# A first feed-forward pass shared by three token tiles instead of two, on eight cores

## The chip, the cores and the metric

The kernel runs on all eight cores of one Trainium2 chip. Each core works on its own two sequences with the same program and nothing is exchanged. The metric is the device time of the slowest core, in microseconds (us).

The runs of these kernels show a second, slower state: in some executions the cores of one die, or of both, show a lower granted TensorE clock and the run is longer (the milder ones 0.92 to 0.94 on one die and about 2990 us, the worst ones 0.81 to 0.82 and about 3300 us, against 2855 us for before in the fast state).

## The reference, cut to what matters

One decoder layer over x of shape (16, 2048, 1024): a half-step SwiGLU feed-forward network (FFN 1), a token mixer (differential attention beside latent attention, one output projection), a second half-step FFN (FFN 2), a final norm. Every part is normed and modulated by shift, scale and gate, which are products of c and `w_ada`.

```python
u = modulate(rmsnorm(h, ffn1_norm[l]), sh1, sc1)
h = h + 0.5 * g1 * swiglu(u, ffn1_w_gate[l], ffn1_w_up[l], ffn1_w_down[l])   # FFN 1
u = modulate(rmsnorm(h, mix_norm[l]), sh2, sc2)
h = h + g2 * hybrid_mixer(u, cos_d, sin_d, cos_r, sin_r, l, ...)              # mixer
u = modulate(rmsnorm(h, ffn2_norm[l]), sh3, sc3)
h = h + 0.5 * g3 * swiglu(u, ffn2_w_gate[l], ffn2_w_up[l], ffn2_w_down[l])   # FFN 2
```

## The kernel before: the parts that the change touches

A core has eight tiles of 512 tokens, numbered 0 to 7. The FFN weights (about 17 MB in bf16 for one FFN) do not stay on chip. They stream through a ring of six buffers `wf`. The first use of a block reads 1 MB of f32 through the POOL queue, converts it on the way and stores a bf16 copy in DRAM; each later use reloads 512 KB.

```python
def load(self, src, scr, key, cols=2048, reuse=True, after=None):
    i = self.i % len(self.bufs); self.i += 1
    buf, res = self.bufs[i], self.res[i]
    if key not in self.seen:                       # first use: f32, POOL queue
        self.seen[key] = Res(f"scr{key}")
        G.dma("pool", f"{self.name}c{i}", 128 * cols * 4, w=[res], after=after, out=buf[:, 0:cols], in_=src[:, 0:cols])
        if reuse:
            G.dma("sp", f"{self.name}s{i}", ..., r=[res], w=[self.seen[key]], out=scr[:, 0:cols], in_=buf[:, 0:cols])
    else:                                          # later: bf16, SP queue
        G.dma("sp", f"{self.name}{i}", 128 * cols * 2, r=[self.seen[key]], w=[res], out=buf[:, 0:cols], in_=scr[:, 0:cols])
    return buf, res
```

Because first loads are slow (8.0 us from issue to landing for a first `w_gu` block on the page of before, 4.9 us for a reload), tiles 0 and 1 go through FFN 1 together (the joint pass): every pair of weight blocks is used for both tiles. Tile 1 borrows memory of the mixer, which is idle then.

```python
def gate_up(fi, hook=None, joint=False):
    sets = [(uF, uFR, ACTV, actR)] + ([(uF1, uF1R, ACT1, act1R)] if joint else [])
    for fp in range(11):                           # 11 feature pairs
        tg, tgR = wf.load(w_gu[fi, fp, 0], ...)
        tu, tuR = wf.load(w_gu[fi, fp, 1], ...)
        for c in range(2):
            for u, uR, av, aR in sets:
                ...                                # 16 matmuls 128x512, then ACT, DVE, DVE
        if hook: hook(fp)                          # modulation blocks, conversions

def down_first(b):
    held = []
    for mp in range(4):
        held.append(down_load(0, mp))              # three w_dn blocks
        down_use(0, mp, held[mp], 0, b, bank=jb)
        if mp < 2: down_use(0, mp, held[mp], 1, b, ACT1, act1R, jb)
    gate.append(G.ops[-1])                         # the mixer's w_in may be loaded
    for mp in (2, 3): down_use(0, mp, held[mp], 1, b, ACT1, act1R, jb)
```

After the joint pass, tile 0 leaves: its mixer input is normed, its state is spilled, tile 2's x is loaded into its place and normed. Then tile 2's FFN 1 and tile 0's mixer run side by side, and so on. Three kinds of side work fill the passes: modulation blocks (`ada`, 1 MB of f32 each, blocks 20 to 23 being the gate of the mixer), conversions of FFN 2's weights ahead of use (`convert`, 1 MB read and 512 KB written each), and the mixer's own first-time weights (`w_in`, `w_uq`, `w_out`).

```python
early = [8, 9, 10, 11, 16, 17, 18, 19, 12, 13, 14, 15]     # modulation blocks in the joint pass
late = list(range(20, 36))
ahead = {3: 5, 4: 5, 5: 5, 6: 5, 7: 5}                      # conversions by tile
def hook_f(x):
    def hook(fp):
        if x == 2 and fp % 2 == 0 and fp < 8 or x > 2 and fp in (1, 5, 8):
            if late: ada(late.pop(0), fb)
        if fp % 2 == 0 and fp // 2 < ahead.get(x, 0): convert([rest.pop(0)])
    return hook
n2(0, A, 1.84, True); n2(1, B, 2.0, True)                   # tiles 0 and 1 leave
load_x(2, A); norm(1, 2, A, 1.95); load_x(3, B)             # (within segments)
```

The numbers 1.84, 2.0 and so on are priorities: a list scheduler in the program fixes each engine's order of instructions at build time, with its own model of durations and transfers.

The softmax here doesn't subtract the row's maximum and nothing guards it: scores larger than these inputs give would overflow.

## Time and profile before

| | before |
|---|---|
| time, median of 4 runs | 2854.95 us (2853.25 to 3221.71; the last one is slow) |
| span of the profiled run, slowest core (7) | 2875.9 us; median of the first die's cores 2845.7 us |
| TensorE busy (core 7) | 2728.7 us, 95% |
| HBM read | 498.70 MB |

These lines are from the page of the profiled run of before: busy time and share of an engine, the span in 40 slices (tenths busy, tenths of full clock, DMA share), the HBM total and the issues of reloads (count, KB of each, us to landing).

```profile
PE 2728.7 (95%) x15753; PEld 1356.6 (47%) x15753; DVE 1492.9 (52%) x2829; ACT 1225.7 (43%) x2034; POOL 599.5 (21%) x565
...
PE   3999789999999999999999999999999999999998
...
PEclk8889999999999999999999999999999999999999
DMA  9678889886885967857547695566564655434553
...
HBM read 498.70 MB, written 112.51 MB: 213 GB/s over the span
...
wf<-s_gu SPq DMA_DIRECT2D x308, 512.0 KB, 4.9
wf<-s_dn SPq DMA_DIRECT2D x106, 512.0 KB, 3.8
...
wf<-s_dn SPq DMA_DIRECT2D x53, 384.0 KB, 3.8
```

TensorE is full nearly everywhere. There are two dents: the first slice (PE is busy for 23.7 of the first 72 us of core 1, while the first weights and x arrive) and slices 5 and 6, where the joint pass hands over to the tile-by-tile part. Core 7 is not the best core to study: cores 6 and 7 had a granted clock of 0.81 from about 76 to 237 us in this run. Core 1 did not. The next lines are the windows view of core 1: from:to, length, busy us of PE, PEld, DVE, ACT and POOL with instruction counts, then the granted clock, the DMA share and GB/s.

```profile
0.00:72.00 72.00, 23.71 (x199) 10.48 (x200) 23.15 (x57) 21.53 (x30) 8.31 (x19) 0.82 0.97 196
72.00:310.00 238.00, 235.40 (x1235) 108.05 (x1234) 94.35 (x147) 50.38 (x78) 26.98 (x46) 0.99 0.88 183
310.00:400.00 90.00, 66.31 (x328) 29.27 (x327) 54.48 (x64) 29.63 (x48) 35.52 (x32) 0.83 0.82 217
400.00:1500.00 1100.00, 1059.28 (x6438) 540.71 (x6436) 598.22 (x1192) 541.52 (x911) 257.62 (x238) 0.99 0.75 211
1500.00:2780.00 1280.00, 1260.61 (x7276) 636.10 (x7275) 699.92 (x1337) 574.22 (x957) 270.43 (x232) 1.00 0.57 183
```

The third line is the handoff: PE is idle for 90.00 − 66.31 = 23.7 us of it. The timeline of PE on core 1 shows why (start, length, instruction, count, and in brackets the idle time before and what ended it):

```profile
318.62 0.79 PE L317 MATMUL psall<-ar,onesf 128*128 128x512 f32 x1 [4.70 <-POOL ar L317]
...
329.74 0.61 PE L317 MATMUL psall<-ft,onesb 128*128 128x512 bf16 x1 [1.96 <-ACT ft L317]
336.99 1.46 PE L317 MATMUL psall<-ft,onesb 128*128 128x512 bf16 x3 [6.64 <-DVE ft L317]
344.55 1.44 PE L317 MATMUL psall<-uF,wf 128*128 128x512 bf16 x3 [6.10 <-ACT uF L317]
```

PE waits for sums of squares in the mixer (`ar`), for the squares of tile 2's x (`ft`), which is still arriving, and then for the normed tile 2 (`uF`).

### The profile page before, as it was taken

Reading aid. Unit: us, or ns where it says so; the run is one execution under the profiler, and the core shown is the slowest. Engines: PE = TensorE matmul, PEld = TensorE weight load, DVE = VectorE, ACT = ScalarE, POOL = GpSimd, SP = SyncE. Lnnn points to the kernel's source line nnn. Section 1 sums busy time; section 2 is a strip of 40 time slices with the busy share of each in tenths; the row PEclk is TensorE's granted clock in tenths of the full one; section 3 lists DMA queues with packets and bytes.
Section 4 is the critical chain, followed back from the end, with each engine's and each line's share of the span. In section 5 each row is a group of like instructions: output and inputs, shape, how many; then the busy total and the mean of one; then the engine's idle time right before and its main releaser. Section 6 shows DMA issues by size and latency. Waiting matters only on the chain.

```text
span 2875.9 us, 40104 instructions; the slowest of 8 cores (2837.4 to 2875.9 us)
## 1 busy us (share of the span) xinstructions
PE 2728.7 (95%) x15753; PEld 1356.6 (47%) x15753; DVE 1492.9 (52%) x2829; ACT 1225.7 (43%) x2034; POOL 599.5 (21%) x565
## 2 busy tenths in 40 slices
PE   3999789999999999999999999999999999999998
PEld 1444344445544454455554444554455545555443
DVE  3333467565546544554336685565654565434443
ACT  3210325335623665246663353464255533566211
POOL 1011220241312203313023123220222212210110
PEclk8889999999999999999999999999999999999999
DMA  9678889886885967857547695566564655434553
GB/s 199 144 153 176 243 187 219 217 242 198 247 240 158 256 184 223 243 177 228 171 145 234 166 268 196 166 207 195 184 187 133 225 173 179 157 125 162 180 184 116
DMA packets 169773, 552.67 MB, mean 192 GB/s; under 512 B 17648, under 2 KB 34416, under 8 KB 160112
## 3 DMA queue, kind: packets, MB, share of 16 engines
q1 hardware_dynamic: 152304, 488.91, 52.8%
q0 software_dynamic: 17280, 61.19, 13.8%
q8 instruction: 125, 2.05, 0.3%
q14 instruction: 64, 0.52, 0.1%
HBM read 498.70 MB, written 112.51 MB: 213 GB/s over the span
## 4 chain that ended last, share of the span: by engine, by line
PE 80%; DVE 10%; DMA 7%; ACT 2%; issue 1%; POOL 1%; SPq 0%; DVEq 0%; POOLq 0%; ACTq 0%
PE psall L317 80%; DMA wf<-s_gu 2%; DMA mix<-w_ada 1%; DVE mt L317 1%; DVE junk L317 1%; DVE pt L317 1%; DVE h L317 1%; DVE bt L317 1%; DVE mix L317 1%; DMA h<-xT 1%; DVE nt L317 1%; DMA s_h<-mt 1%; DVE ft L317 1%; DMA wm<-w_out 1%; DMA wf<-s_dn 1%; DVE rec L317 1%
## 5 line engine op out<-in xcount | busy, mean ns | idle before, releaser
L317 PE MATMUL psall<-uF,wf 128*128 128x512 bf16 x5280 | 1436.9, 384 | 30.1 <-DVE ft L317 9.9
L317 PEld LDWEIGHTS psall<-uF,wf 128*128 128x128 bf16 x5280 | 502.3, 99 | 554.1 <-issue 71.6
L317 PE MATMUL psall<-actv,wf 128*128 128x512 bf16 x2640 | 730.7, 379 | 2.7 <-DMA wf<-s_dn 2.7
L317 ACT ACTIVATE pt<-psall 128x512 bf16<-128x512 f32 (+3 forms) x896 | 488.2, 560 | 366.1 <-PE psall L317 363.2
L317 ACT ACTIVATE ft<-psall 128x512 f32<-128x512 f32 x352 | 209.7, 597 | 635.3 <-PE psall L317 628.5
L317 DVE SCALAR_TENSOR_TENSOR ft<-ft,psall 128x512 f32<-128x512 f32 x352 | 240.2, 684 | 394.4 <-ACT ft L317 393.6
L317 PEld LDWEIGHTS psall<-actv,wf 128*128 128x128 bf16 x2640 | 248.9, 98 | 246.9 <-DMA wf<-s_dn 3.2
L317 PE MATMUL psall<-mix,pt 128*128 128x129 bf16 x3264 | 329.8, 221 | 21.6 <-DVE pt L317 15.8
L317 PEld LDWEIGHTS psall<-mix,pt 128*128 128x128 bf16 x3264 | 248.7, 98 | 215.2 <-DVE pt L317 34.1
L317 DVE TENSOR_TENSOR actv<-ft,psall 128x512 bf16<-128x512 f32 x330 | 226.0, 685 | 230.7 <-PE psall L317 227.9
L317 PE MATMUL psall<-uM,wm 128*128 128x512 bf16 x896 | 302.6, 384 | 6.2 <-ACT mt L317 4.0
L317 POOL TENSOR_TENSOR sq<-h 128x512 f32<-128x512 f32 x175 | 189.9, 1093 | 388.8 <-DVE h L317 375.7
L317 DVE SCALAR_TENSOR_TENSOR h<-psall,SC,h 128x512 f32<-128x512 f32 x128 | 95.9, 749 | 317.4 <-PE psall L317 317.2
L317 POOL TENSOR_TENSOR ac<-h 128x512 f32<-128x512 f32 x25 | 30.1, 1205 | 903.3 <-DVE h L317 596.2
L317 PE MATMUL psall<-mix 128*128 128x512 bf16 x576 | 209.5, 367 | 0.2 <-ACT pt L317 0.2
L317 POOL TENSOR_TENSOR ac<-ac,sq 128x512 f32<-128x512 f32 x150 | 199.0, 1327 | 8.5
L317 DVE TENSOR_TENSOR mt<-tab,psall 128x512 f32<-128x512 bf16 (+1 forms) x208 | 139.6, 683 | 74.2 <-ACT bt L317 55.5
L317 DVE TENSOR_TENSOR nt<-h,rs 128x512 f32<-128x512 f32 x192 | 139.7, 746 | 35.4 <-ACT rs L317 22.8
L317 PE MATMUL psall<-oT,wm 128*128 128x512 bf16 x512 | 150.8, 379 | 0.0
L317 ACT ACTIVATE bt<-psall 128x512 bf16<-128x512 f32 x104 | 61.9, 596 | 201.2 <-PE psall L317 201.0
L317 PEld LDWEIGHTS psall<-uM,wm 128*128 128x128 bf16 x896 | 87.2, 99 | 112.9 <-issue 8.6
L317 PE MATMUL psall<-mix,wf 128*128 128x512 bf16 x528 | 134.6, 413 | 0.0
(98 smaller groups left out, 2180.6 us busy)
## 6 DMA issues: line engine op xcount, KB each, us to landing
wf<-s_gu SPq DMA_DIRECT2D x308, 512.0 KB, 4.9
wf<-s_dn SPq DMA_DIRECT2D x106, 512.0 KB, 3.8
wm<-s_in SPq DMA_DIRECT2D x63, 512.0 KB, 5.0
wf<-w_gu POOLq DMA_DIRECT2D x44, 512.0 KB, 8.0
s_gu<-wf SPq DMA_DIRECT2D x44, 512.0 KB, 7.8
wf<-s_dn SPq DMA_DIRECT2D x53, 384.0 KB, 3.8
s_h<-h SPq DMA_DIRECT2D x16, 1024.0 KB, 6.7
mt<-s_h SPq DMA_DIRECT2D x64, 256.0 KB, 5.2
```

What stands on the lines that cost most here:

```text
L317: ins = getattr(eng, o.fn)(**o.kw)
```

## The change

The intent: let tile 2 join the first pass. Its state and its FFN memory lie in memory that belongs to the mixer's scratch (`mix2`: attention outputs, latents, probabilities, temporaries, rope table), all idle until the pass is over. The weights are then reloaded one pass fewer. In the down pass the tiles leave one by one, so that the first tile's mixer can start while the others still give TensorE work. Four modulation blocks (20 to 23) and four conversions move into the longer joint pass. The core of the diff (memory plan and renames cut):

```diff
         def gate_up(fi, hook=None, joint=False):
-            sets = [(uF, uFR, ACTV, actR)] + ([(uF1, uF1R, ACT1, act1R)] if joint else [])
-            for fp in range(11):
+            sets = [(uF2, uF2R, ACT2, act2R), (uF, uFR, ACTV, actR), (uF1, uF1R, ACT1, act1R)] if joint else [...]
+            steps = [(0, 1)] + [(fp,) for fp in range(2, 11)] if joint else [(fp,) for fp in range(11)]
...
-        def down_first(b):
+        def down_first():
+            sets = [(2, ACT2, act2R), (1, ACTV, actR), (0, ACT1, act1R)]
+            two = Rot([0, 1])
             held = []
             for mp in range(4):
                 held.append(down_load(0, mp))
-                down_use(0, mp, held[mp], 0, b, bank=jb)
-                if mp < 2:
-                    down_use(0, mp, held[mp], 1, b, ACT1, act1R, jb)
-            gate.append(G.ops[-1])
-            for mp in (2, 3):
-                down_use(0, mp, held[mp], 1, b, ACT1, act1R, jb)
+                for slot, av, aR in sets[:3 if mp < 2 else 1]:
+                    down_use(0, mp, held[mp], slot, 0, av, aR, two)
+                if mp == 1:
+                    gate.append(G.ops[-1])
+            for slot, av, aR in sets[1:]:
+                for mp in (2, 3):
+                    down_use(0, mp, held[mp], slot, 0, av, aR, two)
...
-        early = [8, 9, 10, 11, 16, 17, 18, 19, 12, 13, 14, 15]
+        early = [8, 9, 10, 11, 16, 17, 18, 19, 12, 13, 14, 15, 20, 21, 22, 23]
         def hook_j(fp):
-            for i in range(2 if fp == 9 else 1):
-                ada(early.pop(0), jb)
+            for i in range(2 if fp in (2, 4, 5, 7, 8, 10) else 1):
+                if early:
+                    ada(early.pop(0), jb)
+            if fp in (1, 3, 6, 9):
+                convert([rest.pop(0)])
...
-        late = list(range(20, 36))
-        ahead = {3: 5, 4: 5, 5: 5, 6: 5, 7: 5}
+        late = list(range(24, 36))
+        ahead = {4: 5, 5: 6, 6: 6, 7: 5}
...
-                if x == 2 and fp % 2 == 0 and fp < 8 or x > 2 and fp in (1, 5, 8):
+                if x > 3 and fp in (1, 5, 8):
```

More of the change, by code (lines that the diff above doesn't have):

```diff
@@ L413, in build, with part2 @@
         uFR = [Res(f"uF{k}") for k in range(NK)]
-        uM = sb("uM", [128, NK, 512], BF16)
+        mix2 = sb("mix2", [128, 47 * 512], BF16)
+        cut2 = [0]
+        def part2(n, dt=BF16):
+            ap = mix2[:, cut2[0]:cut2[0] + n * 512]
+            cut2[0] += n * 512
+            return ap if dt == BF16 else ap.bitcast(dt)
+        oT = part2(8).rearrange("p (h n) -> p h n", h=8)
+        uM = part2(8).rearrange("p (k n) -> p k n", k=NK)
+        qm = part2(4).rearrange("p (h n) -> p h n", h=4)
+        lat = part2(5).rearrange("p (j n) -> p j n", j=5)
+        ptiles = Rot([(part2(1), Res(f"pt{i}")) for i in range(6)])
+        mtmp = Rot([(part2(2, F32), Res(f"mt{i}")) for i in range(7)])
+        tab, tabR = part2(2).rearrange("p (i n) -> p i n", i=2), Res("tab")
+        ACT2 = mix2[:, 0:22 * 512].rearrange("p (f n) -> p f n", f=22)
+        act2R = [Res(f"act2_{f}") for f in range(22)]
+        uF2 = mix2[:, 38 * 512:46 * 512].rearrange("p (k n) -> p k n", k=NK)
+        uF2R = [Res(f"uF2_{k}") for k in range(NK)]
+        H.append(mix2[:, 22 * 512:38 * 512].bitcast(F32).rearrange("p (k n) -> p k n", k=NK))
+        HR.append([Res(f"h2_{k}") for k in range(NK)])
         uMR = [Res(f"uM{k}") for k in range(NK)]
-        onat = uM[:].rearrange("p k n -> p (k n)").bitcast(F32).rearrange("p (h q d) -> p h q d", h=4, q=4)
+        onat = uM.rearrange("p k n -> p (k n)").bitcast(F32).rearrange("p (h q d) -> p h q d", h=4, q=4)
         ACTV = sb("actv", [128, 22, 512], BF16)
@@ L438, in build @@
         uF1R = [Res(f"uF1_{k}") for k in range(NK)]
-        oT = sb("oT", [128, 8, 512], BF16)
         oTR = [Res(f"oT{h}") for h in range(8)]
-        qm = sb("qm", [128, 4, 512], BF16)
         qmR = [Res(f"qm{h}") for h in range(4)]
-        ptiles = Rot([tile(f"pt{i}", [128, 512], BF16) for i in range(6)])
-        lat = sb("lat", [128, 5, 512], BF16)
         latR = [Res(f"lat{j}") for j in range(5)]
         onatm = lat[:, 0:4, :].rearrange("p j n -> p (j n)").rearrange("p (q h d) -> p q h d", q=4, h=4)
-        tab, tabR = tile("tab", [128, 2, 512], BF16)
         WF = [sb(f"wf{i}", [128, 2048], BF16) for i in range(6)]
@@ L453, in build @@
         ntmp = Rot([tile(f"nt{i}", [128, 512], F32) for i in range(2)])
-        mtmp = Rot([tile(f"mt{i}", [128, 512], F32) for i in range(7)])
         rstmp = Rot([tile(f"rs{i}", [128, 512], F32) for i in range(2)])
@@ L478, in build @@
         colc_sb = con[:, 130:131]
-        lam_t, lamR = mtmp.items[0]
-        lam_sb = lam_t[:, 0:256].rearrange("p (i n) -> p i n", i=4)
         cTR, badaR, gainsR, gsmR, colcR = [Res(n) for n in ("cT", "bada", "gains", "gsm", "colc")]
@@ L494, in build @@
         junk, junkR = tile("junk", [128, 512], BF16)
+        lam_t, lamR = junk[:].bitcast(F32), junkR
+        lam_sb = lam_t.rearrange("p (i n) -> p i n", i=4)
         ident = cm[:, 0, :]
@@ L568, in prologue @@
         def prologue():
-            load_x(0, A, 4)
+            load_x(0, 2, 4)
             G.dma("sp", "c1", 67072, w=[cTR, badaR, gainsR, gsmR, colcR], out=con[:], in_=consts)
@@ L578, in lambdas @@
         def lambdas():
-            G.dma("sp", "c6", 131072, w=[lamR], out=lam_t[:, 0:256], in_=lamv)
+            G.dma("sp", "c6", 131072, w=[lamR], out=lam_t, in_=lamv)
             TT(lam_sb[:, 0, :], lam_sb[:, 0, :], lam_sb[:, 1, :], ALU.mult, [lamR], [lamR])
@@ L598, in mixer_init @@
             transfer(uF1R, qzR)
+            transfer(act2R, oTR + uMR + qmR)
             G.dma("pool", "c0", 3 * 65536, w=[cmR], after=after, out=cm[:].rearrange("p c n -> p (c n)"), in_=cmats)
@@ L723, in gate_up @@
             bank = jb if joint else fb
-            sets = [(uF, uFR, ACTV, actR)] + ([(uF1, uF1R, ACT1, act1R)] if joint else [])
-            for fp in range(11):
-                tg, tgR = wf.load(w_gu[fi, fp, 0], s_gu[fi, fp, 0], ("gu", fi, fp, 0))
-                tu, tuR = wf.load(w_gu[fi, fp, 1], s_gu[fi, fp, 1], ("gu", fi, fp, 1))
-                for c in range(2):
-                    f = 2 * fp + c
-                    for u, uR, av, aR in sets:
+            sets = [(uF2, uF2R, ACT2, act2R), (uF, uFR, ACTV, actR), (uF1, uF1R, ACT1, act1R)] if joint else [(uF, uFR, ACTV, actR)]
+            steps = [(0, 1)] + [(fp,) for fp in range(2, 11)] if joint else [(fp,) for fp in range(11)]
+            for step in steps:
+                tiles = {}
+                for fp in step:
+                    for i in range(2):
+                        tiles[fp, i] = wf.load(w_gu[fi, fp, i], s_gu[fi, fp, i], ("gu", fi, fp, i))
+                for u, uR, av, aR in sets:
+                    for f in range(2 * step[0], 2 * step[-1] + 2):
+                        (tg, tgR), (tu, tuR), c = tiles[f // 2, 0], tiles[f // 2, 1], f % 2
                         bg, bu = bank.next(), bank.next()
@@ L739, in gate_up @@
                 if hook:
-                    hook(fp)
+                    for fp in step:
+                        hook(fp)
         def down_load(fi, mp):
@@ L805, in load_u @@
         def load_u(t):
-            G.dma("sp", "lu", 1048576, r=[s_uR[t]], w=uMR, slack=1500.0, out=uM[:].rearrange("p k n -> p (k n)"), in_=s_u[t])
+            G.dma("sp", "lu", 1048576, r=[s_uR[t]], w=uMR, slack=1500.0, out=uM.rearrange("p k n -> p (k n)"), in_=s_u[t])
         def unspill(t, s):
@@ L1034, in build @@
         begun = [o for o in G.ops if o.dma][-1]
+        with G.seg(-0.95, -0.9, "lam", eng="dve"):
+            lambdas()
         with G.seg(-0.95, -0.9, "st1.0"):
-            st = hstats(A, jb.next())
+            st = hstats(2, jb.next())
         with G.seg(-0.8, -0.8, "N1.0"):
-            apply_norm(A, 0, 0, st, uF, uFR, ntmp)
-        with G.seg(-0.7, -0.7, "x.1", eng="sp"):
-            load_x(1, B, 4, after=begun)
-        with G.seg(-0.2, 0.0, "N1.1"):
-            st = hstats(B, jb.next())
-            apply_norm(B, 0, 0, st, uF1, uF1R, ntmp)
-        with G.seg(0.2, 0.4, "lam", eng="dve"):
-            lambdas()
-            table(0)
-        early = [8, 9, 10, 11, 16, 17, 18, 19, 12, 13, 14, 15]
-        def hook_j(fp):
-            for i in range(2 if fp == 9 else 1):
-                ada(early.pop(0), jb)
-        with G.seg(0.0, 1.333, "F1.0+1g"):
+            apply_norm(2, 0, 0, st, uF2, uF2R, ntmp)
+        for t, s, dst, dstR in ((1, 1, uF, uFR), (2, 0, uF1, uF1R)):
+            with G.seg(-0.7, -0.7, f"x.{t}", eng="sp"):
+                load_x(t, s, 4, after=begun)
+            with G.seg(-0.2, 0.0, f"N1.{t}"):
+                st = hstats(s, jb.next())
+                apply_norm(s, 0, 0, st, dst, dstR, ntmp)
+        early = [8, 9, 10, 11, 16, 17, 18, 19, 12, 13, 14, 15, 20, 21, 22, 23]
+        rest = [("gu", a, b) for a in range(11) for b in range(2)] + [("dn", a, 0) for a in range(12)]
+        def hook_j(fp):
+            for i in range(2 if fp in (2, 4, 5, 7, 8, 10) else 1):
[3 more added lines that the diff above has]
+                convert([rest.pop(0)])
+        with G.seg(0.0, 2.0, "F1.012g"):
             gate_up(0, hook_j, joint=True)
-        with G.seg(1.333, 2.0, "F1.0+1d"):
-            down_first(0)
+        with G.seg(2.0, 3.0, "F1.012d"):
+            down_first()
         gate = gate[0]
-        with G.seg(1.6, 1.9, "mixinit", eng="pool"):
+        with G.seg(2.8, 2.9, "mixinit", eng="pool"):
             mixer_init(gate)
@@ L1061, in n2 @@
             with G.seg(x, x + 0.05, f"N2.{t}"):
-                st = hstats(s, fb.next()) if fast else spread(squares(hsrcs(s), acct, sqt, accr), fb.next(), D, rstmp)
+                st = hstats(s, 2) if fast else spread(squares(hsrcs(s), acct, sqt, accr), fb.next(), D, rstmp)
                 dst, dstR = (ACTV[:, 14:22, :], actR[14:22]) if t else (uM, uMR)
@@ L1081, in norm @@
             with G.seg(lo, lo + 0.05, f"N{2 * i - 1}.{t}"):
-                st = spread(sums, fb.next(), D, rstmp) if sums else hstats(s, fb.next())
+                st = spread(sums, fb.next(), D, rstmp) if sums else hstats(s, 2)
                 apply_norm(s, 2 * i - 2, t // 4, st, uF, uFR, ntmp)
-        order = [(1, t, t % 2) for t in range(2, 8)] + [(2, t, t % 2) for t in range(8)]
-        mixers = [(0, 2.0, 3.0), (1, 3.0, 4.4), (2, 4.4, 6.2), (3, 6.2, 8.3), (4, 8.3, 9.3), (5, 9.3, 10.7), (6, 10.7, 12.5), (7, 12.5, 14.5)]
-        rest = [("gu", a, b) for a in range(11) for b in range(2)] + [("dn", a, 0) for a in range(12)]
-        late = list(range(20, 36))
-        ahead = {3: 5, 4: 5, 5: 5, 6: 5, 7: 5}
+        order = [(1, t, t % 2) for t in range(3, 8)] + [(2, t, t % 2) for t in range(8)]
+        mixers = [(0, 2.75, 3.85), (1, 3.85, 5.1), (2, 5.1, 6.7), (3, 6.7, 8.6), (4, 8.6, 9.6), (5, 9.6, 10.9), (6, 10.9, 12.5), (7, 12.5, 14.4)]
+        late = list(range(24, 36))
+        ahead = {4: 5, 5: 6, 6: 6, 7: 5}
         def hook_f(x):
             def hook(fp):
-                if x == 2 and fp % 2 == 0 and fp < 8 or x > 2 and fp in (1, 5, 8):
+                if x > 3 and fp in (1, 5, 8):
                     if late:
@@ L1099, in hook_f @@
             return hook
-        n2(0, A, 1.84, True)
-        n2(1, B, 2.0, True)
-        with G.seg(1.8, 1.85, "x.2"):
-            load_x(2, A)
-        norm(1, 2, A, 1.95)
-        with G.seg(2.0, 2.05, "x.3"):
-            load_x(3, B)
+        n2(0, 2, 2.68, True)
+        transfer(act2R + HR[2] + uF2R, latR + [tabR] + [res for _, res in ptiles.items + mtmp.items])
+        with G.seg(2.9, 3.0, "tab.0", eng="dve"):
+            table(0)
+        n2(1, 1, 2.84, True)
+        with G.seg(2.85, 2.86, "x.3"):
+            load_x(3, 1)
+        norm(1, 3, 1, 2.95)
+        n2(2, 0, 3.0, True)
+        with G.seg(3.0, 3.05, "x.4"):
+            load_x(4, 0)
+        ra(*mixers[0])
+        ra(*mixers[1])
         for n, (f, t, s) in enumerate(order):
-            x = float(n + 2)
+            x = float(n + 3)
             nxt = order[n + 1] if n + 1 < len(order) else None
@@ L1115, in build @@
                         unspill(nxt[1], nxt[2])
-                    elif nxt[1] > 3:
+                    elif nxt[1] > 4:
                         load_x(nxt[1], nxt[2])
@@ L1119, in build @@
             with G.seg(x, x + 0.667, f"F{f}.{t}g", lead=0.05):
-                gate_up(f - 1, hook_f(n + 2))
-            if n == 0:
-                ra(*mixers[0])
+                gate_up(f - 1, hook_f(n + 3))
             if t == 6 and f == 2:
```

## The prediction

> **What bounds it now.** TensorE. The page's first part gives PE 2728.7 us busy of 2875.9 (95%); the chain of waits puts 80% of the span on PE. A 128x512 matmul takes 0.216 us in the stream (44 in 9.50 us, timeline of the first down pass), 0.262 us where the granted clock is 0.81. So only PE's idle 147 us, and clock, can be won. By the windows view: 48 us idle before 72 us (weights and x arriving), about 27 us at 320 to 380 us (handoff from the joint pass to mixer 0 and tile 2), 13 us at the end, some 59 us over the middle, mostly at tile boundaries with DMA share 0.95 or more.
>
> In the handoff slot 0 is done at 314 us, leaving 19 us of down pass for slot 1. Then PE waits on stats of tile 2's x (last landed near 354 us, held further by slow DVE copies), on w_in (gated until 314 us) and on latent sums. Tile 2's gate starts at 367 us.
>
> **What the change does.**
> 1. A third tile runs in the joint pass. PE's matmuls stay the same; 33 weight reloads go (about 16.5 MB of 553); four conversions and four modulation blocks move into this pass. It gets 114 us longer (528 x 0.216), the rest 114 us shorter. Per feature pair DMA falls from 2.5 MB in 13.8 us to 3.1 MB in 20.7 us; full-clock cores already keep PE full here, so that wins nothing directly.
> 2. Tiles leave the down pass one by one: after the first, 38 us of matmuls remain instead of 19, and w_in is released 19 us before the first exit. Mixer 0's projections mix with the down passes (the program order shows it). But tile 3's x still needs slot 1's spill and norm; that step took about 40 us before. The hole shrinks from 27 to about 10 us: -17 us.
> 3. Startup: in PE's order all eight stat matmuls of the third x stand before the second tile's gate. Before, x parts landed 4.6 us apart, the last at 65.8 us; four more put the start near 78 us, against 24 extra gate matmuls (5 us) done earlier: +6 us.
> 4. The first step covers two feature pairs with four of six buffers; the next pair's second buffer frees only eight matmuls before the step ends, and a w_gu load takes 8.0 us: +4 us. Late weights of the fourth down block: +2 us.
> 5. One tile boundary fewer in the busy middle: -5 us.
>
> Aliasing adds waits (mixer scratch behind the third tile's spill, the rope table later), mostly under PE work.
>
> **Prediction.** 2854.7 - 17 + 12 - 5, about 2845 us; 8 in 10: 2822 to 2872. Faster over 2%: 0.06; within: 0.90; slower: 0.04.
>
> **What would show each step.** PE idle at the start 54 us instead of 48, waiting on ft from late x; one gap of about 4 us on wf<-w_gu some 100 matmuls later; handoff idle about 10 us instead of 27, projections among down matmuls; DMA share in the joint pass about 0.75; 33 weight reloads fewer; PE busy equal at equal clock.
>
> **What would make it wrong.** [...] cores 6 and 7 alone show 0.81, from about 72 to 236 us. If a longer joint pass keeps it, the slowest core loses up to 20 us more. Or the DMA queue at the handoff may keep the hole at 25 us; or the start may be hidden better.

The sum: −17 for the hole, +6 + 4 + 2 = +12 for the start and −5 for the boundary, and 2854.7 − 17 + 12 − 5 came to about 2845 us. The "up to 20 us" was an estimate outside the sum; with the spacings of the trace, 528 × (0.262 − 0.216) gives 24 us. The "slow DVE copies" are two of 64x512, 6.05 us together on core 7 (from 354.16 us). "Keep PE full" is 235.40 us busy of 238.00 on core 1.

## The result, and the profile after

| | before | after |
|---|---|---|
| time, median of 4 runs | 2854.95 us | 2816.31 us (2813.38 to 2818.09) |
| ratio of the fast runs | | 0.9866, 95% interval 0.9846 to 0.9885 |
| PE busy (each slowest core) | 2728.7 us | 2698.9 us |
| first die, median of its cores, profiled run | 2845.7 us | 2804.5 us |

All ratios here are the mean time of one kernel's fast runs over the mean time of the other's fast runs of the same rounds, so they are not quite the ratio of the medians quoted. The gain is about 38 us, 1.3%: inside "within 2%", but below the range of the prediction (2822 to 2872), which had 10 us. The same lines of the page after:

```profile
PE 2698.9 (96%) x15767; PEld 1351.5 (48%) x15767; DVE 1486.7 (53%) x2837; ACT 1209.5 (43%) x2026; POOL 558.5 (20%) x535
...
PE   3899999999998999999999999999999999999998
...
PEclk8899999999999999999999999999999999999999
DMA  9587668878768878786456765656555745445553
...
HBM read 481.92 MB, written 112.51 MB: 211 GB/s over the span
...
wf<-s_gu SPq DMA_DIRECT2D x286, 512.0 KB, 4.9
wf<-s_dn SPq DMA_DIRECT2D x99, 512.0 KB, 4.2
...
wf<-s_dn SPq DMA_DIRECT2D x49, 384.0 KB, 4.0
```

The dent at the handoff has gone, the DMA digits of the joint pass (slices 2 to 6) have fallen from 6 to 8 to 5 to 8, and there are 22 + 7 + 4 = 33 reloads fewer. The windows of core 1 after, cut at the matching places:

```profile
0.00:84.00 84.00, 36.53 (x231) 15.34 (x232) 27.20 (x59) 32.59 (x46) 7.78 (x18) 0.92 0.86 190
84.00:430.00 346.00, 338.95 (x1788) 156.44 (x1786) 135.97 (x212) 67.42 (x104) 39.92 (x61) 1.00 0.71 157
430.00:520.00 90.00, 86.69 (x425) 41.15 (x424) 72.28 (x109) 47.52 (x80) 26.60 (x26) 0.99 0.89 244
520.00:1500.00 980.00, 957.79 (x5989) 496.77 (x5988) 542.18 (x1119) 502.76 (x856) 226.55 (x210) 1.00 0.73 214
1500.00:2740.00 1240.00, 1219.33 (x7079) 616.62 (x7077) 689.82 (x1310) 551.00 (x930) 258.57 (x220) 1.00 0.58 182
```

PE busy sums to 2645 us before and 2639 us after, so the work did not change; only idle time and clock did. The handoff window (third line) has 90.00 − 86.69 = 3.3 us idle instead of 23.7, at a clock of 0.99 instead of 0.83, although it moves more bytes (244 GB/s at a share of 0.89). A few lines of PE's timeline on core 1 after, in the handoff:

```profile
429.47 0.50 PE L317 MATMUL psall<-ar,onesf 128*128 128x512 f32 x1 [0.69 <-POOL ar L317]
429.81 0.82 PE L317 MATMUL psall<-mix,wf 128*128 128x512 bf16 x3
430.47 0.38 PE L317 MATMUL psall<-mix,wm 128*128 128x512 bf16 x1
430.68 0.59 PE L317 MATMUL psall<-mix,wf 128*128 128x512 bf16 x2
...
449.58 0.38 PE L317 MATMUL psall<-bt,cm 128*128 128x512 bf16 x1 [1.34 <-DVE mix L317]
```

Projections of mixer 0 (`mix,wm`) and down matmuls of the tiles that are still in the pass (`mix,wf`) alternate. The wait for `ar` that cost 4.70 us before costs 0.69 us here, and the longest gap is 1.34 us. No matmul of core 1 between 430 and 520 us has the spacing of 0.427 us; between 310 and 400 us of before 21 had it.

**Where the time went.** To compare kernels at equal work I gave each matmul of a trace the spacing that it has in an undisturbed stream (the traces show 0.216 us for 512 columns, 0.109 for 256, 0.056 for 128) and subtracted the sum of these from its real start, counted from PE's first matmul. The rest is time lost: idle, or at a granted clock below 1.00 (0.50 and 0.81 above). The table has the median over the cores (cores with a complete trace, without 6 and 7 of before), by stretch of work. The first stretch is the start, the second holds the handoff and the tile after it, the third is the rest of FFN 1 and the first mixers.

| us lost in work from, to | 0–200 | 200–500 | 500–1200 | 1200–2700 |
|---|---|---|---|---|
| before | 27.3 | 50.2 | 41.4 | 31.0 |
| after (first chip) | 34.3 | 8.6 | 27.6 | 34.2 |
| after (another chip, `r_after`) | 36.2 | 11.2 | 30.3 | 35.0 |

So the start lost 7 to 9 us more, about as predicted (10 at the start itself). The handoff and the next tile lost about 40 us less, where I had 17. The middle lost 11 to 14 us less, where I had 5.

### The profile page after: what moved, and what is told of

Same layout as the page of the kernel before. It is cut to its first block, busy times and chain, and to the rows that moved or that the text cites. A ratio compares the mean times of both kernels' runs of the same rounds, so it can differ in the third digit from the quotient of the medians.

```text
span 2816.6 us, 40097 instructions; the slowest of 8 cores (2792.1 to 2816.6 us)
## 1 busy us (share of the span) xinstructions
PE 2698.9 (96%) x15767; PEld 1351.5 (48%) x15767; DVE 1486.7 (53%) x2837; ACT 1209.5 (43%) x2026; POOL 558.5 (20%) x535
## 4 chain that ended last, share of the span: by engine, by line
PE 83%; DVE 7%; DMA 7%; ACT 2%; issue 1%; SPq 0%; POOL 0%; DVEq 0%; POOLq 0%
PE psall L317 83%; DVE mix L317 3%; DMA h<-xT 2%; DMA wf<-s_gu 1%; DMA mix<-w_ada 1%; DVE nt L317 1%; DVE h L317 1%; DMA s_h<-h 1%; DMA wf<-w_gu 1%; DVE junk L317 1%; DMA wf<-w_dn 1%; DVE rec L317 1%; ACT mix L317 0%; DVE ft L317 0%; ACT uF L317 0%
## 5 line engine op out<-in xcount | busy, mean ns | idle before, releaser
L317 PE MATMUL psall<-uF,wf 128*128 128x512 bf16 x4928 | 1369.4, 380 | 14.8 <-DMA wf<-s_gu 7.5
L317 ACT ACTIVATE mix<-psall 128x512 bf16<-128x512 f32 (+5 forms) x1064 | 578.3, 552 | 496.2 <-PE psall L317 481.4
L317 PE MATMUL psall<-mix 128*128 128x129 bf16 (+2 forms) x4160 | 583.8, 251 | 21.6 <-DVE mix L317 19.8
L317 PE MATMUL psall<-mix,wm 128*128 128x512 bf16 x1536 | 522.0, 379 | 2.9 <-DVE mix L317 1.8
L317 PEld LDWEIGHTS psall<-mix 128*128 128x128 bf16 x4160 | 327.8, 98 | 289.4 <-DVE mix L317 49.7
L317 PE MATMUL psall<-mix,wf 128*128 128x512 bf16 x1056 | 247.7, 388 | 11.6 <-DMA wf<-w_gu 7.5
L317 PEld LDWEIGHTS psall<-mix,wm 128*128 128x128 bf16 x1536 | 149.8, 98 | 180.4 <-issue 4.3
L317 DVE TENSOR_TENSOR mix<-mix,psall 128x512 f32<-128x512 bf16 (+1 forms) x208 | 139.2, 683 | 63.7 <-ACT bt L317 54.8
L317 PEld LDWEIGHTS psall<-mix,wf 128*128 128x128 bf16 x1056 | 103.9, 100 | 140.4 <-issue 13.4
L317 PE MATMUL psall<-wm,mix 128*128 128x256 bf16 (+1 forms) x576 | 144.5, 284 | 0.9 <-DVE mix L317 0.9
```

The lines of the kernel that those rows point to most:

```text
L317: ins = getattr(eng, o.fn)(**o.kw)
```

## The experiments

Four theories of why the handoff gave so much:

- Order: the tiles leave one by one, so matmuls remain to cover the handoff.
- Early `w_in`: the mixer's first weights are released before the first exit.
- Room: tile 3, the first single tile, has no side transfers, since they went into the joint pass.
- Ready input: any kernel that has the next tile's input ready at the end of the down pass would have gained the same; the third tile is not needed.

Four runs came first. All were slow on the second die, so here only the median of the first die's cores is used, averaged over the runs in which that die was not slow. The kernel before had 2860.3 us there. That die was not quite at its best either: its mean clock for before was 0.977. So small differences of these four runs weigh little.

**`e1_together`**, the changed kernel with all three tiles leaving together:

```diff
-                for slot, av, aR in sets[:3 if mp < 2 else 1]:
+                for slot, av, aR in sets:
                     down_use(0, mp, held[mp], slot, 0, av, aR, two)
...
-            for slot, av, aR in sets[1:]:
-                for mp in (2, 3):
-                    down_use(0, mp, held[mp], slot, 0, av, aR, two)
```

> The changed kernel, but all three tiles stay together to the end of the joint down pass (every block for all three tiles in turn), so the first tile is complete 19 us before the last matmul of the pass instead of 38 us. Theory 1 (the gain is cover at the handoff): 15 to 25 us of the 38 us come back, so about 2835 us, with PE idle for over 15 us just after the joint pass. Rival, theory 2 (the gain is that transfers, four conversions and four modulation blocks, left the crowded tile-by-tile part): within 5 us of the changed kernel, 2814 to 2821 us.

Measured: 2839.4 us, still 21 us below before. The same kernel was run again, with five fast runs of before:

> The same kernel as e1_together (all three tiles stay together to the end of the joint down pass), run again since that chip was in the slow state. On e1's undisturbed die it kept about 23 us of a gain of about 44. Theory 1 in its reduced form (the order of leaving is about half of the gain): ratio to the kernel before 0.991 to 0.994, about 20 us slower than the changed kernel.

**`e1b_together`**: ratio 0.9875 (0.9828 to 0.9923), against 0.986 for the changed kernel on other chips. It lost 18.1 us in the second stretch, against 8.6 and 11.2. So the order of leaving is worth about 7 to 9 us in the trace and no more in time. It is not the main part.

**`e2_before_early_win`**, the kernel before with `w_in` released after the second down block, 19 us earlier:

```diff
-            gate.append(G.ops[-1])
...
+                if mp == 1:
+                    gate.append(G.ops[-1])
```

> The kernel before, with one line moved: the mixer's input weights are released after the second down block (19 us before the first tile is complete) instead of when it is complete. Rival, theory 3 (the hole was the late weights): about 2840 us, the hole at 320 to 370 us shrinks by 12 us or more. Theory 1 (the hole is missing cover while the next tile's x and norm arrive): 2850 us or more, hole about as before.

Measured: 2864.2 us on the quiet die, 4 us above before. Its counterpart **`e8_late_win`**, the changed kernel with `if mp == 3:` in place of `if mp == 1:`, ran beside a repeat of the changed kernel:

> The changed kernel with the mixer's input weights released only when the first tile has left the down pass, not after the second down block. Theory 1 with cover alone (the 38 us of remaining down matmuls are what counts): at most 4 us slower. Theory 1 with both needed (the cover is used up by projections, and these need the weights): 8 to 15 us slower, PE waiting on the w_in tiles while slot 1 and slot 0 run.

> The changed kernel as it is, so that the other runs of this set can be compared with it on the same chip. If the chip is in the fast state: 2813 to 2819 us; on an undisturbed die its cores should have a median about 40 us below those of the kernel before.

Measured: `e8_late_win` 0.9858 (0.9839 to 0.9877), `r_after` 0.9859 (0.9840 to 0.9879). The early release is worth nothing either way; this theory falls.

**`e3_nomove`** and **`e4_before_move`** separate the moved side work from the third tile. `e3` is the changed kernel with the four modulation blocks and the four conversions put back into the first single tile; `e4` is the kernel before with them moved into its joint pass.

```diff
# e3, against the changed kernel
-        early = [..., 20, 21, 22, 23]
+        early = [...]
-            for i in range(2 if fp in (2, 4, 5, 7, 8, 10) else 1): ...
-            if fp in (1, 3, 6, 9): convert([rest.pop(0)])
+            for i in range(2 if fp == 9 else 1): ada(early.pop(0), jb)
-        late = list(range(24, 36)); ahead = {4: 5, 5: 6, 6: 6, 7: 5}
+        late = list(range(20, 36)); ahead = {3: 4, 4: 5, 5: 6, 6: 6, 7: 5}
-                if x > 3 and fp in (1, 5, 8):
+                if x == 3 and fp % 2 == 0 and fp < 8 or x > 3 and fp in (1, 5, 8):
+            if n == 0: ra(*mixers[0]); ra(*mixers[1])    # recorded later: they need blocks 20 to 23
# e4: the reverse of this, in the kernel before
```

> The changed kernel, with the four conversions of second-pass weights and the four modulation blocks put back from the joint pass into the following tiles. Theory 2 (relief of the transfers): 10 to 15 us slower than the changed kernel, about 2828 us, the loss between 500 and 900 us. Theory 1: at most 4 us slower, about 2818 us.

> The kernel before, with only that move made: four conversions and four modulation blocks taken into its joint pass of two tiles. Theory 2: about 2843 us. Theory 1: within 5 us of the kernel before, 2850 to 2859 us, or slower, as its joint pass already has a DMA share near 0.9.

Measured: `e3` 2847.6 us, 12.7 below before; it lost 39.3 us in the second stretch. `e4` 2869.7 us, 9 us above before. Its joint pass had a DMA share of 0.95 on core 1 (before 0.88), PE waited 10.4 us in it for `w_gu` loads (before none), and its start stretch lost 41.0 us instead of 27.3. So with two tiles the joint pass has no room for the whole move, and with three tiles the move matters. But `e3` also changes where the mixers are recorded, so cleaner versions followed. They leave the joint pass alone and only pull side work that the changed kernel does later forward into tile 3: **`e9_ada4`** four modulation blocks, **`e7_conv4`** four conversions, **`e6_crowd`** both.

```diff
# e9 and e6
-                if x > 3 and fp in (1, 5, 8):
+                if x == 3 and fp % 2 == 0 and fp < 8 or x > 3 and fp in (1, 5, 8):
# e7 and e6
-        ahead = {4: 5, 5: 6, 6: 6, 7: 5}
+        ahead = {3: 4, 4: 5, 5: 5, 6: 5, 7: 3}
```

> The changed kernel with four modulation blocks in tile 3, the first tile after the joint pass, as the kernel before has in its first tile; no conversions there. e6_crowd, with four conversions besides, was 33 us slower than the changed kernel. If that tile's transfers are the limit whatever their kind: 12 to 18 us slower than the changed kernel, and conversions are the rest. If the conversions alone did it (they also store): within 4 us.

> The changed kernel with the four conversions alone in tile 3. If any transfer counts by its size: a load of the same size and a store besides, so 15 to 22 us slower; if the modulation blocks alone did it: within 4 us.

> The changed kernel with four conversions and four modulation blocks moved from later tiles into tile 3, the first tile after the joint pass, which has none in the changed kernel. The joint pass and the order at the handoff stay. Theory 2 in its narrow form (the first tile after the joint pass gains because its transfers are few): 8 to 14 us slower than the changed kernel, lost in the 200 us after the joint pass. Theory 1: at most 4 us slower.

Measured, with the loss in work 200 to 500 (changed kernel 8.6 to 11.2):

| | ratio to before | lost in 200–500 |
|---|---|---|
| `e9_ada4` | 0.9924 (0.9876 to 0.9972) | 31.7 us |
| `e7_conv4` | 0.9945 (0.9897 to 0.9993) | 38.2 us |
| `e6_crowd` | 0.9982 (0.9949 to 1.0016) | 39.8 us |

Four blocks of 1 MB in tile 3 cost as much as half of the whole gain, and eight cost nearly all of it. So side work in tile 3 costs what the theory of room says, and more than I expected of `e6` (8 to 14 us). Through what does it cost this? **`e11_dummy`** has only the transfers: four plain copies of 1 MB of f32, stored as 512 KB of bf16 in spare DRAM, at the moments when the blocks of `e9` are loaded, without matmuls or ring buffers. **`e12_slots`** has only the rest: ring buffers and small matmuls as in `e9`, but 8 KB loaded for each block (the sums go to a spare tile, so the output stays right).

```diff
# e11
+                if x == 3 and fp % 2 == 0 and fp < 8:
+                    G.dma("pool", "spare", 1048576, w=[spareR], after=wf.res[wf.i % 6].rs[-1], out=spare, in_=w_ada[24 + fp // 2])
# e12: slots() is ada() with in_=w_ada[j][:, 0:16] and the sum kept in a spare tile
+                if x == 3 and fp % 2 == 0 and fp < 8:
+                    slots(24 + fp // 2, fb)
```

> The changed kernel with four plain 1-MB transfers of the POOL queue more in tile 3, at the places where the four modulation blocks of the earlier run stand, but into spare DRAM: no matmuls, no buffer of the FFN weight ring. The four modulation blocks cost about 20 us (ratio 0.9924 against 0.986). If the cost is the transfer (the first-time loads of mixer 0's weights stand behind it in the same queue[...]): ratio 0.991 to 0.995, 12 to 25 us lost in the 100 us of work after the joint pass. If it is the ring's buffers: ratio 0.985 to 0.988, under 5 us lost there.

> The changed kernel with four ring buffers and 64 small matmuls taken in tile 3 as four modulation blocks take them, but each loaded by 8 KB only (the sums go to a spare tile, the output stays right). If the cost of about 20 us is the transfer: ratio 0.985 to 0.988, under 5 us lost in the 100 us of work after the joint pass. If it is the ring's buffers (fewer gate weights ahead): ratio 0.990 to 0.995, 10 to 25 us lost there.

Measured: `e11` 0.9933 (0.9905 to 0.9961), and 36.7 us lost in the second stretch, 5 us more than with the real blocks. `e12` had only two fast runs, 2833.58 us and a profiled one with a die at 0.98 of the clock, so its ratio is unclear; cores 5 to 7, which were undisturbed, lost 18.2 us in the second stretch, 7 to 10 us more than the changed kernel. So adding the copies costs more than adding the ring buffers; the two together are more than the real blocks cost, so they are not shares of one sum. Windows of core 5 from 480 to 580 us, first the changed kernel, then `e11`, then `e12`:

```profile
480.00:530.00 50.00, 50.00 (x282) 25.49 (x281) 36.19 (x82) 22.67 (x43) 15.69 (x16) 1.00 0.84 222
530.00:580.00 50.00, 49.93 (x321) 26.22 (x319) 40.63 (x117) 29.60 (x54) 1.62 (x2) 1.00 0.79 222
```

```profile
480.00:530.00 50.00, 43.24 (x214) 19.98 (x213) 35.49 (x63) 18.86 (x36) 21.24 (x21) 0.93 1.01 257
530.00:580.00 50.00, 42.87 (x279) 21.99 (x278) 37.13 (x123) 22.56 (x46) 0.00 (x0) 1.00 0.79 218
```

```profile
480.00:530.00 50.00, 45.23 (x253) 21.92 (x251) 37.80 (x45) 14.98 (x29) 20.05 (x21) 1.00 0.87 245
530.00:580.00 50.00, 48.95 (x332) 25.70 (x331) 39.74 (x144) 24.74 (x54) 0.00 (x0) 1.00 0.75 206
```

With the copies the DMA share goes from 0.84 to 1.01 in the first window and stays at 0.79 in the second; PE is idle for 6.8 and 7.1 us in these two windows, and no single wait of PE between 430 and 620 us is longer than 3.2 us. The issues on the POOL queue of core 5 between 430 and 620 us (KB written, median us from issue to landing) show which loads land later, first the changed kernel, then `e11`:

```profile
wm<-w_out POOLq DMA_DIRECT2D x4, 512.0 KB, 7.2
...
wm<-w_uq POOLq DMA_DIRECT2D x2, 384.0 KB, 8.3
```

```profile
wm<-w_out POOLq DMA_DIRECT2D x4, 512.0 KB, 11.9
...
spare<-w_ada POOLq DMA_DIRECT2D x3, 512.0 KB, 10.3
wm<-w_uq POOLq DMA_DIRECT2D x2, 384.0 KB, 12.9
```

The first-time weights of mixer 0, which pass through the same queue just then, land 4.6 to 4.7 us later each, in a stretch that holds the 50 us at a DMA share of 1.01. But late loads are not what PE waited for. These are lines of the waits view of PE in `e11` (core 5, 430 to 620 us: who waited for what, us in total, times, longest):

```profile
PE psall L317 <- DVE mix L317: 7.7, 8, 3.2
PE psall L317 <- ACT mix L317: 3.6, 11, 0.8
PE psall L317 <- DVE bt L317: 2.4, 1, 2.4
...
PE psall L317 <- DMA wm<-w_in: 0.8, 1, 0.8
```

Of some 18 us of waits only 0.8 us end on a transfer; the others end on VectorE, ScalarE and, for 0.3 us, GpSimd, mostly on work of mixer 0 itself. In the changed kernel the same view lists 3.4 us of waits, none of them on a transfer. What differs is the order of PE's instructions, since the list scheduler plans with modelled transfer times, so every added transfer changes it. Between 400 and 500 us of work the changed kernel places the gate matmuls of tile 3 among those of mixer 0 in groups of 2.3 on average; `e12` has groups of 5.2, `e9` of 5.3, `e11` of 21 and `e7` of 28. As I read it, where the groups are long, mixer 0's chain of small steps has few matmuls left to cover its waits. `e9`, too, lost its 31.7 us at a DMA share of 0.85 from 430 to 580 us on core 5, the same as the changed kernel. So the scheduler's order is a rival for the whole loss in tile 3, and the waits speak for it; but the length of the groups alone does not give the loss (`e12` lost 8.3 us there, `e9` 21). No run has the new order without the copies, or the copies in the old order, so the shares stay open.

**`e13_two_ready`** and **`e14_two_ready_move`** test the last theory. Two tiles go jointly as before, but in the changed memory plan: tile 0 sits in the mixer's scratch, so tile 2's x is loaded and normed during the joint pass and its gate matmuls stand ready. `e13` leaves the side work as before; `e14` also moves the four modulation blocks into the joint pass.

```diff
# e13, against the changed kernel
-            sets = [(uF2, ...), (uF, uFR, ACTV, actR), (uF1, ...)] if joint else [...]
+            sets = [(uF2, ...), (uF1, ...)] if joint else [...]
-            steps = [(0, 1)] + ...
+            steps = [(fp,) for fp in range(11)]
+        with G.seg(0.7, 0.7, "x.2", eng="sp"):
+            load_x(2, 0)
+        with G.seg(1.4, 1.42, "N1.2"):              # between gate and down pass
+            st = hstats(0, 2); apply_norm(0, 0, 0, st, uF, uFR, ntmp)
-            sets = [(2, ACT2, act2R), (1, ACTV, actR), (0, ACT1, act1R)]
+            sets = [(2, ACT2, act2R), (1, ACT1, act1R)]
... early, late, ahead, order and mixers as in the kernel before
# e14, against e13
+        early = [..., 20, 21, 22, 23]; late = list(range(24, 36)), none of them in tile 2
```

> Two tiles jointly as before, but in the changed memory plan: tile 0 in the mixer's memory, so tile 2's x is loaded and normed during the joint pass and its gate stands ready; 33 reloads and four modulation blocks stay as before. Theory A, the hole was a wait for tile 2's input and ready work fills it: handoff loss 35 falls to about 10, ratio 0.988 to 0.992. Rival B, the hole needs the third tile in the joint pass, because mixer 0's first-time weight loads and tile 2's reloads then collide: the loss only moves into tile 2's stretch, ratio 0.996 to 1.002.

> As the last one, with the four modulation blocks of tile 2 moved into the joint pass. If the move and ready work are what counts together: ratio 0.985 to 0.990, 3 to 8 us below the last one. If a two-tile joint pass has no room for the transfers (0.88 of the queues' time busy before): it loses 8 us or more there and comes out level with the last one or slower.

Measured: 0.9993 (0.9965 to 1.0021) and 0.9990 (0.9967 to 1.0014). The theory of ready input falls as the whole cause. Core 1 from 310 to 340 and from 340 to 400 us, before and then `e13`:

```profile
310.00:340.00 30.00, 12.69 (x37) 3.85 (x35) 18.64 (x19) 11.87 (x20) 22.85 (x19) 0.66 0.95 287
340.00:400.00 60.00, 53.62 (x291) 25.43 (x292) 35.84 (x46) 17.76 (x28) 12.68 (x14) 0.91 0.76 182
```

```profile
310.00:340.00 30.00, 27.58 (x139) 11.84 (x137) 21.95 (x37) 17.42 (x26) 6.25 (x8) 1.00 0.97 265
340.00:400.00 60.00, 47.22 (x237) 22.39 (x236) 43.48 (x51) 17.56 (x26) 27.33 (x27) 0.89 0.70 170
```

The first part of the hole is filled (27.58 us busy of 30 instead of 12.69), but part of it comes back in the next window, where tile 1 leaves and mixer 0 runs (PE is idle for 12.8 us there instead of 6.4). Over the second stretch `e13` lost 46.8 us and `e14` 38.5, against 50.2 of before, and both gave 5 to 9 us back at the start (32.7 and 36.3 against 27.3). Neither lost less in the third stretch (41.1 and 41.9), so the gain there goes with the third tile too. In these two kernels the four blocks did not matter to the tile behind the handoff: in work 300 to 500 `e13` lost 24.2 us and `e14` 25.5, and `e4`, also without them, 14.4 against 13.7 of before.

**`e5_start` and `e10_start2`** mend the start of the changed kernel: the third tile's norm is recorded among the second tile's gate matmuls, so that its stat matmuls no longer stand in front of them. `e5` keeps all modulation blocks and two of the four conversions in the joint pass; `e10` gives the third tile's squares buffers of their own and drops the four conversions there (it also plans with a later third x; that line and the hook of `e5` are cut here).

```diff
# e10, against the changed kernel
+        def third():
+            st = hstats(0, jb.next(), btmp)          # e5: without btmp
+            apply_norm(0, 0, 0, st, uF1, uF1R, ntmp)
...
+                        if third and f == 1 and u is uF:   # e5: f == 2
+                            third()
...
-            for i in range(2 if fp in (2, 4, 5, 7, 8, 10) else 1): ...
-            if fp in (1, 3, 6, 9): convert([rest.pop(0)])
+            for i in range(2 if 1 < fp < 10 else 0): ada(early.pop(0), jb)
...
+        ahead = {4: 6, 5: 6, 6: 6, 7: 6}
```

> The changed kernel with its two startup costs taken out: the statistics of the third x are recorded after the first gate matmuls of the second tile, and the next pair's weights take the two free buffers before any modulation block does. If the start costs what I predicted (waits on ft for the third x, then a gap on the w_gu load), it is 7 to 12 us faster than the changed kernel, about 2806 us in the fast state. If the start is bound by the arrival of the weights and x as a whole, within 3 us.

> The changed kernel with its startup mended as in e5_start, but without that run's new loss at the end of the joint gate pass: no modulation block in the last feature pair, no conversions in the joint pass (six in each of tiles 4 to 7), statistics of the third x in buffers of their own. 6 to 10 us faster than the changed kernel, ratio to before about 0.983; if the conversions now crowd tiles 4 to 7, only 0 to 4 us.

Measured: `e5` 0.9872 (0.9845 to 0.9899), no gain. It lost 6 us less at the start and got a new wait on `wf<-w_dn` (3.9 us on core 1) at the end of the gate pass. `e10` 0.9834 (0.9787 to 0.9882), 2813.15 to 2815.55 us, with 27.0 us lost at the start, as little as before. To see whether that counts in time, both kernels ran in the same rounds:

> The version with the start mended (third tile's norm among the first gate matmuls, no conversions in the joint pass), now in the same rounds as the changed kernel. If the lost time at the start (36.4 us against 27.2 us at equal work) counts in full: 6 to 10 us below the changed kernel, ratio 0.982 to 0.985 to the kernel before. If it is given back later: within 2 us of the changed kernel.

> The changed kernel in the same rounds, for the direct difference. Both theories expect its ratio to the kernel before at 0.985 to 0.988, as twice before.

On that chip the first die had a median granted clock of 0.974 to 0.980 in all fast runs of before, and the gain of the changed kernel came out smaller than expected: 0.9901 (0.9881 to 0.9921). By the medians it gained 30 us on that die and 37 on the other. `e10b` had only two runs that count as fast, 2838.29 and 2839.58 us, against 2838.89 to 2849.26 us of the changed kernel. The second die was undisturbed in most runs of both. The mean of the median of its cores, over the runs in which it was not slow, is 2799.0 us for `e10b` (5 runs), 2806.2 us for the changed kernel (6) and 2843.2 us for before (10). So the mended start, with the conversions out of the joint pass, is worth about 7 us on that die, more than the scatter (the means are known to about 1 us each). On die 0 the difference of the medians is 5 us, and in the time of the slowest core it is not shown.

## Why the prediction was wrong, point by point

**The step that failed** is point 2: "The hole shrinks from 27 to about 10 us: -17 us." Its mechanism was partly right, its size was not. In idle time the hole went from 23.7 to 3.3 us on core 1; in time lost at equal work it went from 35.1 us (work 200 to 300) to 7.5 and 10.5 us (work 300 to 400, medians of the two chips). Three things were missing in the sum.

1. *The hole cost more than its idle time.* I counted 27 us of PE idle. At equal work, before lost 35.1 us between 200 and 300 us of work. On core 1 it was 36.5 us, of which 26.3 us are gaps; the 21 matmuls at a spacing of 0.427 us instead of 0.216 add 21 × (0.427 − 0.216) = 4.4 us, and other matmuls at the granted clock of 0.50 and short waits the rest. The trace of before showed this clock of 0.50 in the hole of core 1 (316.5 to 323.2 and 326.7 to 350.5 us); in the handoff after no matmul of core 1 has that spacing. My sum had no term for it.
2. *The loss went on in the next tile.* Before lost another 14 us between 300 and 500 us of work, where tile 2 ran beside mixer 0's first-time weight loads and four modulation blocks. After, the tile at that place lost 0.8 us. This was in no term.
3. *The other half of the change counts too.* I costed the moved side work at nothing: "full-clock cores already keep PE full here, so that wins nothing directly". In the joint pass that is true (core 1 after is busy for 338.95 of 346.00 us). With three tiles it counts one tile later: with the four blocks back in tile 3 the second stretch loses 31.7 us, with the conversions 38.2, with both 39.8. (Whether through the transfers or through the order that the scheduler makes with them is open; see `e11`.) And the order of leaving and the early `w_in`, to which I gave the 17 us, are worth 7 to 9 us and nothing. The two halves need each other: with two tiles the joint pass has no room for the whole move (`e4`, 9 us slower, at a DMA share of 0.95), with three tiles it has (0.71). But the four blocks do not explain the 14 us that before lost in its own tile 2, for `e4` lost as much there without them. The cause of these 14 us stays open.

The sum, with the medians of the table (after: mean of the two chips): hole 35 to 10, −25; the tile after it, 14 to 1, −13 to −15; start +8; the middle −12; the end +4. That makes about −39, and 38 to 40 us were measured.

**What was right.**

- The start: +6 for the stat matmuls and +4 for the first step's buffers were forecast; 7 to 9 us were lost, with both marks in the trace. (The +2 for late weights of the fourth down block showed as waits of 3.3 us on `w_dn` on core 1, none on core 5.) These lines of core 1 after are two of the waits on the third tile's squares, and the one on `w_gu` (forecast about 4 us):

```profile
72.92 1.04 PE L317 MATMUL psall<-ft,onesb 128*128 128x512 bf16 x2 [2.30 <-ACT ft L317]
76.04 1.04 PE L317 MATMUL psall<-ft,onesb 128*128 128x512 bf16 x2 [2.08 <-ACT ft L317]
112.47 5.11 PE L317 MATMUL psall<-mix,wf 128*128 128x512 bf16 x16 [3.06 <-DMA wf<-w_gu]
```

- 33 reloads fewer, projections among the down matmuls, PE's work unchanged, a DMA share of 0.71 in the joint pass (forecast 0.75).
- The middle: −5 forecast for one tile boundary, −11 to −14 measured; direction right, half the size.
- The risk that a longer joint pass keeps the 0.81 clock did not come true: in the profiled run after, cores 0 to 3 had it for some 5 us at a time (at 464 us, cores 0 and 1 again at 1420 us) and the others never (mean clocks 0.990 to 0.996). In the profiled run of before only cores 6 and 7 were granted 0.81, from about 76 to 237 us of the joint pass, while cores 4 and 5 of the same die were at 1.00 from 120 to 236 us. Nor does this 0.81 of before explain the gain, since the medians of the undisturbed die fell from 2845.7 to 2804.5 us.

**What was wrong beside it.** The range. I treated the terms as independent and gave the largest one no spread upwards.

## What to carry to other kernels

Cost an idle stretch by start times at equal work, not by idle time: here the matmuls at a granted clock of 0.50 around the gaps (4.4 us for 21 of them on core 1) and the loss in the stretch behind it (14 us) belong to it. When a change makes room for transfers in a phase that is already full of matmuls, look for the gain also where those transfers are taken away, and test it by putting them back there. Where a program schedules itself with a model of transfers, compare the order of PE's instructions and what ends PE's waits before blaming the transfers: here the copies changed both, and the waits ended on other engines. Four blocks or four conversions back in tile 3 lost 20 to 27 us more in the trace, and the four plain copies of `e11` about 25 us more (36.7 against 11.2 us); how much of the loss is the program's changed order is open.
